# A norm's sum of squares: the last two squares added on VectorE, and the sums one matmul group later

## The chip, the cores and the metric

The kernel runs on one core of one Trainium2 chip. Its engines are TensorE (PE; its weight loads are listed as PEld), VectorE (DVE), ScalarE (ACT), GpSimd (POOL) and SyncE (SP, which here only issues DMAs). The metric is the device time of one execution in microseconds (us), lower being better, as the median of several runs.

## The reference, cut to what matters

The kernel computes a two-layer decoder trunk in float32 for 512 tokens of width 1024. Each layer is a half-step SwiGLU feed-forward, a mixer, and a second half-step feed-forward. Layer 0 mixes with a state-space head group beside an mLSTM head group, layer 1 with sparse attention. Every one of the six stages begins with an RMS norm over the 1024 features of a token.

```python
def rms_norm(x, g):
    xf = x.astype(jnp.float32)
    y = xf * lax.rsqrt(jnp.mean(xf * xf, axis=-1, keepdims=True) + EPS) * g
    return y.astype(x.dtype)

def swiglu(h, w_gate, w_up, w_down):
    return (jax.nn.silu(h @ w_gate) * (h @ w_up)) @ w_down

for l in range(DEPTH):                        # DEPTH = 2
    x = x + 0.5 * swiglu(rms_norm(x, ffn_norm[l, 0]), ...)
    h = rms_norm(x, mix_norm[l])
    m = hybrid_mixer(h, ...) if l % 2 == 0 else sparse_attention(h, ...)
    x = x + m
    x = x + 0.5 * swiglu(rms_norm(x, ffn_norm[l, 1]), ...)
```

## The kernel before, in words

The residual x lives on chip, transposed: `xT` has the features on the 128 partitions in eight chunks (k = 0 to 7) of 512 tokens. Float32 products are made of three matmuls each (`mm3`, lines 241 to 243) over a high and a low part of both operands. Weights come by DMA into a ring of raw buffers; ScalarE and VectorE make their high and low parts ("form", lines 361 and 363), or ScalarE and an accumulating DMA from GpSimd's queue do (lines 391 to 393). TensorE reads the forms and sets the ring free again.

**Stages.** The order is ffn00, mix0, ffn01, ffn10, mix1, ffn11. A feed-forward works on 11 units of 256 hidden features. Its first two units (`unit`) are plain products: eight groups of 12 matmuls of 512 columns. The first four groups take the chunks 0 to 3 (gate, gate, up, up), the last four the chunks 4 to 7. The other units (`unit_seven`) use a seven-product scheme over sums and differences of blocks of x (tile `xf`, made by `xforms`).

**The norm, spread over the end of one stage and the start of the next.** The matmuls of the next stage are begun on x times gain, not yet divided by its root mean square; the division is a multiplication of the results by a row `rrow`. For each of the six norms but the first (which is taken from x as it is loaded), the steps are:

- `prep_later`, called as each pair of chunks of the new x is finished, in the order (0, 1), (2, 3), (6, 7), (4, 5), at the end of mix1 in the order 0 to 7. Per chunk ScalarE makes the high part (line 657), VectorE the low part (line 660) of tile `xgn`, and ScalarE squares the chunk (line 669) into tile `ssq`. GpSimd adds the squares of all but the last pair into one partial sum (through `vtt`, line 356). The squares of the last two chunks stay as they are: with GpSimd's sum there are three partial sums.
- `settle_later`, first call: `sums` (line 327) adds over partitions and over the partial sums with matmuls against a column of ones: for each of the four blocks of 128 tokens one matmul per partial sum, into tile `pssq`. A float32 matmul of this kind is two records in the profile. VectorE then takes the mean (line 624), GpSimd raises it to the power -0.5 (line 626).
- `settle_later`, second call: `rows_of` (line 336, tile `prow`) turns the four columns into a row on every partition, ScalarE copies it to `rrow` (line 630). `xforms` (line 444) and the units' results wait for `rrow`.

**Where the two calls stand.** In `unit` after the second and the fourth group of 12 matmuls (line 600; ffn00 is the "late" case, whose norm has no sums). In mix0 (`unit_eight`) ahead of the second and the third group. In mix1 one call alone, after the first four jobs of the indexer: attention uses the column, not the row.

**The order.** Every step is added to a `Plan` with an engine and an estimated cost; the plan places the steps of the whole kernel by list scheduling (earliest start, then longest way to the end) and so fixes each engine's order. TensorE's steps keep their written order within a stream; only the mixers have several streams, which the plan interleaves. VectorE, ScalarE, GpSimd and SyncE may take later steps first. The plan counts 0.2 + 0.45 us per partial sum for `sums`, and 0.15 + 1.05e-3 us per element of a row for a VectorE step.

Of the kernel before, what the change touches and what calls it, by code (L numbers as in the profile page):

```python
# [13 lines left out]
ALU = mybir.AluOpType  # L14
# [4 lines left out]
NB = T // P  # L19
# [194 lines left out]
class Trunk:  # L214
# [135 lines left out]
    def t(self, us, issue, reads, writes):  # L350
        self.plan.add("tensor", us, issue, reads, writes)
# [224 lines left out]
    def unit(self, raws, stream, late, summed):  # L576

        nc, rrow = self.nc, self.rrow  # L580
        ps = self.pair("pg", "pA"), self.pair("pu", "pB")
        f = []
        for qs in ((0, 1), (2, 3)):
            for i in range(4):
                for _ in range(2 if not f else 1):
                    next(stream, None)
                xg, xgk = self.xg, self.xgk
                if len(f) < 4:
                    f.append(self.made(raws[i], i >= summed))
                j, b = f[i]  # L590
                for s in range(2):
                    col = slice(s * P, (s + 1) * P)
                    for q in qs:
                        k = 2 * q + i % 2
                        self.times(
                            *ps[i // 2], s, (j, lambda b=b, q=q, col=col: (b[:, 0, q, col], b[:, 1, q, col])),
                            lambda k=k: (xg[0][k], xg[1][k]), xgk(k), q == 0 and i % 2 == 0, q == 3 and i % 2 == 1, False, T,
                            0.693,
                        )
                if 2 * qs[0] + i in ((2, 4) if late else (1, 3)):  # L600
                    self.settle_later()
        yield
        t, tk = self.place()
        g = lambda: t()[:, 4:8].rearrange("p (s a) b -> p s (a b)", s=2)
        h = lambda: t()[:, 0:4].rearrange("p (s a) b -> p s (a b)", s=2)
        r = lambda: rrow.unsqueeze(1).to_broadcast([P, 2, T])
        gk, hk = ([tk(a + i) for i in range(4)] for a in (4, 0))
        pk = lambda ps: [(*ps[1], 0), (*ps[1], 1)]
        self.vtt(2 * T, g, ps[0][0], r, ALU.mult, gk, pk(ps[0]) + ["rrow"])
        self.s(2 * T, lambda: nc.scalar.activation(g(), g(), AF.Silu), gk, gk, AF.Silu)  # L610
        self.vtt(2 * T, h, ps[1][0], r, ALU.mult, hk, pk(ps[1]) + ["rrow"])
        self.vtt(2 * T, h, h, g, ALU.mult, hk, hk + gk)
        yield t, tk
# [20 lines left out]
    def prep_later(self, which, k, last, squares=True, half=None):  # L634

        nc = self.nc
        if k == 0 and not half:  # L640
            self.which = which
            self.xgn = [[Lazy(lambda: self.part.tile([P, 4, T], F32R, name="xgn", tag="xg")) for _ in range(2)] for _ in range(2)]
            squares4 = Lazy(lambda: self.tmp.tile([P, 4, T], F32, name="ssq", tag="ssq", bufs=1))
            self.sqs = [lambda i=i: squares4()[:, i] for i in range(4)]
            self.ssq = self.sqs[0]
            self.ssqs, self.ssqk = [(self.ssq, 0)], ["ssq"]
            self.xg = [LazyFeat(t) for t in self.xgn]
            self.xgk = lambda k: [("xg", which, i, k) for i in range(2)]
        xgn, xT, ssq = self.xgn, self.xT, self.ssq
        halves = (0, 1) if half is None else (half,)  # L650
        cols = slice(halves[0] * H, halves[-1] * H + H)
        n = cols.stop - cols.start
        for j in (k, k + 1):
            g, x = self.gain(which, j), xT[:, j, cols]
            hi, lo = (lambda i=i, j=j: xgn[i][j // 4]()[:, j % 4, cols] for i in range(2))
            hik, lok = ([("xg", which, i, j)] for i in range(2))
            self.s(n, lambda hi=hi, x=x, g=g: nc.scalar.activation(hi(), x, AF.Copy, scale=g), self.xk(j, halves), hik)

            def low(hi=hi, lo=lo, x=x, g=g, j=j):
                nc.vector.scalar_tensor_tensor(lo(), x, g, hi().bitcast(F32), op0=ALU.mult, op1=ALU.subtract)  # L660

            self.v(n, low, self.xk(j, halves) + hik, lok)
            if not squares:
                continue
            if j == 0:
                sq, sk = ssq, ["ssq"]
            else:
                sq, sk = self.sqs[1 + j % 3], [("sq", j % 3)]
            self.s(n, lambda x=x, sq=sq: nc.scalar.activation(sq()[:, cols], x, AF.Square), self.xk(j, halves), sk)
            if last:  # L670
                self.ssqs, self.ssqk = self.ssqs + [(sq, halves[0] * NB // 2)], self.ssqk + sk
            elif j:
                part = [lambda x=x: x()[:, cols] for x in (ssq, sq)]
                self.vtt(n, part[0], *part, ALU.add, ["ssq"], ["ssq"] + sk, True)
        if last:
            self.pending = 1 + squares

# [1285 lines left out]
```

## Time and profile before

| what | value |
|---|---|
| median of 3 runs | 2012.17 us (2010.16 to 2013.01) |
| profiled execution, its own time | 2003.96 us |
| span of the profiled execution | 2002.2 us |
| mean granted TensorE clock | 0.992 |
| busy: PE, DVE, ACT, POOL | 1956.5, 1627.8, 1264.7, 325.0 us |
| sums (`pssq`) | 120 records, 14.5 us |
| GpSimd's additions of squares, 128x512 | 22, mean 1551 ns |

The span runs from the first to the last instruction on the core. Busy time of an engine is the time in which one of its instructions ran; "idle before" is time that the engine spent waiting just ahead of an instruction, with the one that released it. The granted clock is the share of TensorE's full rate that its clock gate let through. A line number is the line of the kernel where the instruction was issued; where a helper issues for many places, the tile's name tells them apart.

### The profile page before, as it was taken

The page shows a single profiled execution, that of the slowest core. Times are in us where ns is not written, and L with a number is a line of the kernel's source. Part 1 is how long each engine was busy: PE and PEld are TensorE (multiplying, and loading weights), DVE is VectorE, ACT ScalarE, POOL GpSimd, SP SyncE. Part 2 cuts the span into 40 slices and gives each one's busy share as a digit, 9 for nine tenths or more (in the row PEclk, how much of TensorE's full clock was granted, in tenths as well). Part 3 has the DMA queues.
Part 4 walks back from the last instruction along what each step waited for, and adds up shares of the span by engine and source line. Part 5 has one row for each costly group of instructions (what it writes and reads, how often), then busy time and mean ns, then how long its engine had stood idle before and what let it go on. Part 6 is the DMA issues. An engine that isn't in the chain of part 4 may idle for free.

```text
span 2002.2 us, 36425 instructions
## 1 busy us (share of the span) xinstructions
PE 1956.5 (98%) x14674; PEld 1813.3 (91%) x14674; DVE 1627.8 (81%) x2373; ACT 1264.7 (63%) x1906; POOL 325.0 (16%) x401
## 2 busy tenths in 40 slices
PE   8999999999999999999999999999999999999998
PEld 6999999799888888999998999999866588999998
DVE  6888888887888558989788998878589647988886
ACT  6666656567777545766566566666747744757564
POOL 1000002222234110000012001001414521101010
PEclk9999999999999999999999999999899999999999
DMA  8566766467769342666654466565735202666564
GB/s 221 137 157 152 176 155 161 118 166 190 198 176 262 86 117 74 162 172 162 158 149 141 111 170 161 155 174 137 188 88 116 53 17 69 158 158 169 148 170 115
DMA packets 226609, 292.89 MB, mean 146 GB/s; under 512 B 15036, under 2 KB 196488, under 8 KB 225928
## 3 DMA queue, kind: packets, MB, share of 16 engines
q1 hardware_dynamic: 200728, 199.30, 32.2%
q0 software_dynamic: 25632, 91.24, 24.2%
q8 instruction: 115, 1.88, 0.4%
q14 instruction: 54, 0.44, 0.1%
q10 hardware_dynamic: 80, 0.02, 0.0%
HBM read 192.96 MB, written 6.33 MB: 100 GB/s over the span
## 4 chain that ended last, share of the span: by engine, by line
PE 76%; DVE 8%; DMA 8%; issue 5%; ACT 1%; POOL 1%; SPq 0%; POOLq 0%; ACTq 0%; DVEq 0%
PE pA L242 9%; PE pA L241 9%; PE pA L243 9%; PE pD L241 5%; PE pD L243 5%; PE pD L242 5%; DMA form<-raw 3%; PE hm L242 2%; PE hm L243 2%; PE hm L241 2%; PE pB L241 2%; PE pB L243 2%; PE pB L242 2%; DMA raw<-in_hy_w_in 2%; DVE raw L356 2%
## 5 line engine op out<-in xcount | busy, mean ns | idle before, releaser
L363 DVE TENSOR_TENSOR form<-raw,form 128x1024 fp32r<-128x1024 f32 (+2 forms) x382 | 454.9, 1195 | 101.5 <-ACT form L361 100.0
L361 ACT ACTIVATE form<-raw 128x1024 fp32r<-128x1024 f32 (+2 forms) x382 | 392.1, 1030 | 206.0 <-DVE raw L356 142.4
L392 POOL DMA_DIRECT2D form<-raw x172 | 150.9, 879 | 1344.3 <-ACT form L391 1298.3
L356 DVE TENSOR_TENSOR raw<-raw 128x1024 f32<-128x1024 f32 (+2 forms) x281 | 333.2, 1190 | 22.8 <-DMA raw<-in_ffn_w_down 9.0
L241 PE MATMUL pA<-xf,form 128*128 128x256 f32 x1152 | 321.2, 279 | 0.0
L243 PE MATMUL pA<-xf,form 128*128 128x256 f32 x1152 | 320.7, 278 | 0.0
L242 PE MATMUL pA<-xf,form 128*128 128x256 f32 x1152 | 320.7, 278 | 0.0
L391 ACT ACTIVATE form<-raw 128x1024 fp32r<-128x1024 f32 (+1 forms) x172 | 178.2, 1037 | 161.6 <-PE pD L243 74.4
L241 PEld LDWEIGHTS pA<-xf,form 128*128 128x128 f32 x1152 | 217.2, 188 | 0.3
L243 PEld LDWEIGHTS pA<-xf,form 128*128 128x128 f32 x1152 | 217.3, 189 | 0.0
L242 PEld LDWEIGHTS pA<-xf,form 128*128 128x128 f32 x1152 | 217.0, 188 | 0.2
L242 PE MATMUL pA<-hid,form 128*128 128x256 f32 x704 | 198.2, 282 | 3.3 <-DVE hid L363 3.3
L241 PE MATMUL pA<-hid,form 128*128 128x256 f32 x704 | 198.0, 281 | 0.6 <-ACT hid L361 0.5
L243 PE MATMUL pA<-hid,form 128*128 128x256 f32 x704 | 197.2, 280 | 0.0
L393 ACT ACTIVATE form<-raw 128x1024 fp32r<-128x1024 f32 (+1 forms) x172 | 176.5, 1027 | 0.0
L241 PE MATMUL pD<-xf,form 128*128 128x256 f32 x576 | 160.3, 278 | 0.0
L243 PE MATMUL pD<-xf,form 128*128 128x256 f32 x576 | 160.2, 278 | 0.0
L242 PE MATMUL pD<-xf,form 128*128 128x256 f32 x576 | 160.2, 278 | 0.0
L356 DVE TENSOR_TENSOR ft<-ft 128x256 f32<-128x256 f32 (+2 forms) x296 | 151.3, 543 | 3.6
L242 PEld LDWEIGHTS pA<-hid,form 128*128 128x128 f32 x704 | 132.4, 188 | 5.2 <-DVE hid L363 5.1
L241 PEld LDWEIGHTS pA<-hid,form 128*128 128x128 f32 x704 | 132.6, 188 | 1.4 <-ACT hid L361 0.7
L508 ACT ACTIVATE ft<-pA 128x512 f32<-128x512 f32 x120 | 71.5, 595 | 97.7 <-PE pA L243 90.0
(441 smaller groups left out, 5427.6 us busy)
## 6 DMA issues: line engine op xcount, KB each, us to landing
form<-raw POOLq DMA_DIRECT2D x156, 512.0 KB, 5.9
raw<-in_ffn_w_gate SPq DMA_DIRECT2D x88, 512.0 KB, 3.9
raw<-in_ffn_w_up SPq DMA_DIRECT2D x88, 512.0 KB, 4.1
raw<-in_ffn_w_down SPq DMA_DIRECT2D x64, 512.0 KB, 4.0
raw<-in_hy_w_in SPq DMA_DIRECT2D x44, 512.0 KB, 4.7
raw<-in_ffn_w_down SPq DMA_DIRECT2D x32, 384.0 KB, 3.1
raw<-in_hy_w_out SPq DMA_DIRECT2D x16, 512.0 KB, 4.2
form<-raw POOLq DMA_DIRECT2D x16, 384.0 KB, 4.2
```

The costliest lines, as they stand in the source:

```text
L241: mm(out, l[0], r[0], start=start, stop=False)
L242: mm(out, l[0], r[1], start=False, stop=False)
L243: mm(out, l[1], r[0], start=False, stop=stop)
L356: (self.p if pool else self.v)(n, lambda: e.tensor_tensor(out(), x(), y(), op=op), reads, writes)
L361: self.s(n, lambda: nc.scalar.activation(hi(), src(), AF.Copy), srck, hik)
L363: n, lambda: nc.vector.tensor_tensor(lo(), src(), hi().bitcast(F32), op=ALU.subtract), srck + hik, lok
L391: self.s(n, lambda: nc.scalar.activation(f()[:, 1], raw, AF.Copy, scale=-1.0), rawk, lok)
L392: self.plan.add("gpsimd", 0.85, lambda: nc.gpsimd.dma_start(f()[:, 1], raw, accum_op=ALU.add), rawk + lok, lok, 5.5)
L393: self.s(n, lambda: nc.scalar.activation(f()[:, 0], raw, AF.Copy), rawk, hik)
L508: self.s(T, lambda: nc.scalar.activation(to(), ps()[:, :, 0:H], AF.Copy), [(*psk, 0), (*psk, 1)], tok)
```

## The change

With the last pair, VectorE adds each of the two squares to GpSimd's partial sum as it comes (`vtt` with its last argument false is a VectorE step). `ssqs` then holds one partial sum, and `sums` makes four matmuls in place of twelve, in all five planned norms. In `unit` the first call of `settle_later` moves from after the second group to after the third; the second call stays after the fourth. mix0, mix1 and ffn00 keep the places of their calls.

```diff
@@ unit
-                if 2 * qs[0] + i in ((2, 4) if late else (1, 3)):
+                if 2 * qs[0] + i in ((2, 4) if late else (2, 3)):
                     self.settle_later()
@@ prep_later
             self.s(n, lambda x=x, sq=sq: nc.scalar.activation(sq()[:, cols], x, AF.Square), self.xk(j, halves), sk)
-            if last:
-                self.ssqs, self.ssqk = self.ssqs + [(sq, halves[0] * NB // 2)], self.ssqk + sk
-            elif j:
+            if j:
                 part = [lambda x=x: x()[:, cols] for x in (ssq, sq)]
-                self.vtt(n, part[0], *part, ALU.add, ["ssq"], ["ssq"] + sk, True)
+                self.vtt(n, part[0], *part, ALU.add, ["ssq"], ["ssq"] + sk, not last)
```

## The prediction

> **What bounds the kernel now.** I read the page's busy line and the chain that ended last first, to see whose time counts.
>
> ```profile
> PE 1956.5 (98%) x14674; PEld 1813.3 (91%) x14674; DVE 1627.8 (81%) x2373; ACT 1264.7 (63%) x1906; POOL 325.0 (16%) x401
> ...
> PE 76%; DVE 8%; DMA 8%; issue 5%; ACT 1%; POOL 1%; SPq 0%; POOLq 0%; ACTq 0%; DVEq 0%
> ```
>
> TensorE (PE) is busy 98% of the span and carries 76% of the chain. The other engines feed it through rings of buffers that PE itself sets free, so time taken out of PE's queue should move the end, unless a feeder is late afterwards. VectorE (DVE) at 81% is the next candidate.
>
> Next PE in order of time around the sums of the five planned norms (tile pssq) and the row transposes (prow) that follow; the first row is the tile's own (min/median/max ns), each other one is from a stretch of its own: start, us, instruction, and in brackets PE's wait ahead of it. I call the norms A (mix0), B (ffn01), C (ffn10), D (mix1), E (ffn11).
>
> ```profile
> L327 PE MATMUL pssq<-raw,ssq x120: 164/250/352, 359.1 to 1664.4; 128*128 128x1 f32 x120
> 359.12 2.73 PE L327 MATMUL pssq<-raw,ssq 128*128 128x1 f32 x24
> 366.14 0.38 PE L336 MATMUL prow<-raw 128*128 128x128 f32 x2
> 750.17 2.73 PE L327 MATMUL pssq<-raw,ssq 128*128 128x1 f32 x24
> 758.36 0.49 PE L336 MATMUL prow<-raw 128*128 128x128 f32 x3
> 1085.14 2.74 PE L327 MATMUL pssq<-raw,ssq 128*128 128x1 f32 x24
> 1093.30 0.38 PE L336 MATMUL prow<-raw 128*128 128x128 f32 x2
> 1429.89 2.73 PE L327 MATMUL pssq<-raw,ssq 128*128 128x1 f32 x24
> 1432.88 0.40 PE L241 MATMUL gm<-iw,xgn 128*128 128x292 f32 x1 [0.25 <-DVE raw L624]
> 1661.16 3.55 PE L327 MATMUL pssq<-raw,ssq 128*128 128x1 f32 x24 [0.88 <-POOL ssq L356]
> 1672.62 0.38 PE L336 MATMUL prow<-raw 128*128 128x128 f32 x2
> ```
>
> The 12 matmuls of a norm (four token blocks, three partial sums) are 24 records, 2.73 us. The last record lasts 0.25 us and overlaps what follows, so one costs PE (2.73 - 0.25) / 23 = 0.108 us. E took 3.55 us after a wait of 0.88 for GpSimd. And the same work after the sums is not equally long: from their end to prow B has 24 matmuls of 512 columns in 758.36 - 752.90 = 5.46 us, C 5.42, but E 24 in 1672.62 - 1664.71 = 7.91, and A 12 in 366.14 - 361.85 = 4.29 (half of 5.46 is 2.73). So I asked for the granted clock in windows of 3.41 us, the length of the drops, all instructions first:
>
> ```profile
> core 0: us, PE busy (x) PEld busy (x) DVE busy (x) ACT busy (x) POOL busy (x), PEclk, DMA share, GB/s
> 359.19:362.60 3.41, 3.41 (x29) 3.27 (x28) 0.34 (x2) 0.00 (x0) 0.48 (x1) 1.00 0.98 304
> 362.60:366.01 3.41, 3.41 (x10) 2.62 (x9) 0.00 (x0) 0.00 (x0) 0.56 (x1) 0.50 0.19 47
> 1430.97:1434.38 3.41, 3.16 (x26) 3.07 (x27) 0.22 (x2) 0.45 (x3) 1.03 (x1) 1.00 1.09 189
> 1434.38:1437.80 3.42, 2.63 (x12) 2.28 (x11) 2.85 (x8) 1.57 (x5) 2.22 (x2) 0.50 0.95 257
> 1437.80:1441.21 3.41, 3.41 (x17) 3.39 (x15) 1.52 (x2) 1.65 (x3) 3.41 (x8) 0.50 1.04 396
> 1659.67:1663.08 3.41, 2.54 (x24) 2.33 (x22) 2.60 (x5) 2.83 (x5) 1.43 (x1) 1.00 0.41 138
> 1663.08:1666.49 3.41, 3.41 (x14) 3.02 (x14) 0.61 (x2) 0.00 (x0) 1.02 (x1) 0.50 0.02 5
> 1666.49:1669.90 3.41, 3.41 (x10) 2.64 (x9) 0.00 (x0) 0.00 (x0) 0.00 (x0) 0.50 0.00 0
> 611.77:615.18 3.41, 1.08 (x10) 0.88 (x8) 3.41 (x3) 3.41 (x8) 3.33 (x4) 1.00 1.06 281
> 615.18:618.60 3.42, 3.20 (x21) 2.87 (x22) 3.42 (x4) 2.05 (x3) 2.11 (x2) 0.50 1.03 329
> ```
>
> The same windows for pssq alone (length, PE, PEld and VectorE busy, granted clock, DMA share, GB/s):
>
> ```profile
> 359.19:362.60 3.41, 2.66 (x24) 2.57 (x23) 0.16 (x1) 1.00 0.98 304
> 748.29:751.71 3.42, 1.54 (x15) 1.72 (x15) 0.00 (x0) 1.00 0.05 8
> 1086.18:1089.60 3.42, 1.70 (x16) 1.61 (x15) 0.16 (x1) 1.00 0.85 270
> 1430.97:1434.38 3.41, 1.66 (x15) 1.57 (x15) 0.16 (x1) 1.00 1.09 189
> 1659.67:1663.08 3.41, 1.92 (x18) 1.93 (x18) 0.00 (x0) 1.00 0.41 138
> ```
>
> Read together: in a window in which one-column sums and waits of PE fill 2.66 us (A), 1.66 + 0.25 = 1.91 (D) or 1.92 + 0.87 = 2.79 (E), the next stretch is granted half the clock. Where they fill 1.54 (B) or 1.70 (C), nothing follows: B's and C's 24 matmuls took 5.46 and 5.42. A plain wait does the same (611.77: 2.33 idle, then 0.50). So, as a reading of these rows: over about half a window of one-column matmuls or waiting costs at least one window at half speed. Sums of 2.73 us can do that alone if they lie in one window.
>
> **The change part by part.**
>
> *Sums of 4 instead of 12 matmuls, five times.* 16 records less: 16 x 0.108 = 1.73 us per norm, 5 x 1.73 = 8.6 us, all PE time. In E the last six records ran at half speed; there the sums go from 3.55 to about 8 x 0.108 + 0.14 = 1.0, some 0.8 more: 9.4 together.
>
> *The half-clock windows after the sums.* Shortened sums fill 0.9 us of 3.41, far under the 1.70 that did nothing. A gets back 4.29 - 2.73 = 1.6, E 7.91 - 5.42 = 2.5. In D both windows hold 2.63 + 3.41 = 6.04 us of PE work at half speed, so at most 3.0 comes back; at least 0, since PE waits there for other engines too; I take 2.0, nearer to the upper end since PE is full in the second window. Together 6.1.
>
> *Two additions per norm on VectorE.* Priced by the same operation of the same size, 0.69 us (first row: its group, busy us and mean ns; then rows in order of time from A and C):
>
> ```profile
> L356 DVE TENSOR_TENSOR ft<-ft 128x512 f32<-128x512 f32 x112 | 73.8, 686 | 1.0
> 356.72 2.34 DVE L363 TENSOR_TENSOR form<-raw,form 128x1024 fp32r<-128x1024 f32 x2
> 357.04 0.62 ACT L669 ACTIVATE ssq<-raw 128x512 f32<-128x512 f32 x1
> 1087.91 0.16 DVE L624 TENSOR_SCALAR raw<-pssq 128x4 f32<-128x4 f32 x1
> 1088.15 1.47 POOL L626 TENSOR_TENSOR raw<-raw 128x4 f32<-128x4 f32 x1 [5.58 <-DVE raw L624]
> ```
>
> Ten of them are 6.9 us of VectorE. They wait for GpSimd's last addition and for the last square, and the sums now wait for them. Behind them on VectorE stand the low parts of the last chunks and the next weight forms, which PE needs one group (2.73 us) later or more. In A the position of the sums stays: the last square ends at 357.66, VectorE does two forms until 359.06, PE wants the sums at 359.12. If the planner puts the addition between the forms it costs nothing; behind both, 359.06 + 0.69 - 359.12 = 0.63 us. I take half, 0.3. In D the low parts are long done and VectorE idles, so nothing. In the feed-forwards the sums come 12 matmuls (2.73 us) later, which covers 2 x 0.69; in E this also removes the 0.88 us wait for GpSimd, since PE goes on with the third group: -0.9. Without that cover each feed-forward would pay up to 1.4.
>
> *Sums a group later in B, C, E.* No DMA and no new instruction moves: the matmuls, the VectorE step L624 and GpSimd's L626 come later, in no queue of SP. prow stays where it is, so the cover of the chain from sums to prow falls from 24 matmuls (5.46) to 12 (2.73). The slowest chain seen is C: the sums end at 1087.88, L626 at 1088.15 + 1.47 = 1089.62, 1.74 us. That leaves 1.0 us of slack. If L624 stands behind one form of 1.17 us (half of 2.34), PE waits 0.2; behind two, 1.4. Behind a waiting prow stands the second half of the unit. I take 0.2 for each of three: +0.6, range 0 to 4.2.
>
> *Sum:* -9.4 - 6.1 - 0.9 + 0.3 + 0.6 = -15.5 us. Norm A's gain (3.4) comes ahead of mix0's waits for weights; the feeders are released by PE and should move with it, but I leave half of it out as absorbed: +1.5. Forecast **-14 us**. The sum belongs to the profiled execution (span 2002.2, its own time 2003.96); the median of the runs shown, 2012.17, lies 8.2 above, and I carry the difference over: 2012.17 - 14 = **1998.2 us**.
>
> [...]
>
> **The rivals.**
>
> 1. *Only the matmuls go.* The windows lie anywhere against the program; in the timed runs the sums may straddle two windows as B and C do here, or the removed drop reappears at the next wait. For it: two of five norms show no drop. Against: the three others do. Time: -9.4 - 0.9 + 0.9 = -9.4, 2002.8. [...]
>
> 2. *The mixers absorb it.* PE's lead in A and D ends at the next transfer or VectorE chain. Then only B, C and E count: 2 x 1.73 + 1.73 + 0.9 - 0.6 = -5.5, 2006.7. For it: the waits below; against: those feeders wait for buffers that PE sets free.
>
> 3. *The shorter cover is too short.* L624 or the additions stand behind two forms in B, C and E, 1.4 us each, and drops stay elsewhere: -9.4 - 0.9 + 0.3 + 4.2 = -5.8 at worst; with two additions late by 1.4 each time as well, -1.6, 2010.6: no change.
>
> 4. *Slower: the planner draws another order.* It places every step by its own costs; it counts 1.55 us for the sums before and 0.65 after, and has ten more steps to place, so its clock shifts by about 0.9 us per norm. In the mixers several PE streams interleave by that clock, and there PE's longest waits stand:
>
> ```profile
> PE hc L1308 <- DVE rw L1297: 4.9, 2, 2.6
> ...
> PE hm L243 <- DMA form<-raw: 4.0, 4, 1.5
> PE pq L1521 <- DVE q L1511: 3.7, 2, 3.0
> PE gm L242 <- DVE iw L363: 3.4, 1, 3.4
> ```
>
> These are 16.0 us, and the waits over 2.3 us cost a half-speed window (1.7) each. A worse order that doubles them adds 16.0 + 3 x 1.7 = 21: 2012.17 - 14 + 21 = 2019. It decides from 14 + 4 = 18 us of new waits. Against it: PE's order in the feed-forwards is written, and a lead common to all streams leaves their order alone.
>
> **How the numbers follow.** Forecast 0.47, rival 1 0.25, rival 2 0.11, rival 3 0.09, rival 4 0.08. A measurement of this kernel can tell about 0.2%, 4 us. Forecast, rivals 1 and 2 are faster: 0.83; rival 3 is the same, 0.09; rival 4 slower, 0.08. The forecast's own range is 1994 to 2001 (D's window 0 to 3, A's gain whole or half, prow's waits). With rivals 1 and 2 and most of 3 it reaches up to 2009; down to 1992, if in the timed runs four or five norms lose a window.
>
> **What would show it.** Right: pssq x40, about 0.9 us a norm; granted clock 1.00 in the windows after each; 24 matmuls between sums and prow become 12 with prow not waiting; no wait for ssq in E; two more VectorE additions of 0.69 us per norm. Wrong: a wait of prow on L626 or of pssq on VectorE over 1 us, half-clock windows at other places in equal number, or longer waits in mix0 and mix1 than the 16 us above.

## The result, and the profile after

The changed kernel is faster by 0.8%: median 1995.55 us (13 runs, 1990.74 to 2002.94) against 2013.01 for the kernel before on the same chip (13 runs, 1998.89 to 2017.5), ratio 0.992 with a 95% interval of 0.9902 to 0.9937. The forecast was 1998.2 us, 14 us less than before.

The profiled executions differ by less: spans 2002.2 and 1993.7, that is 8.5 us. The one before is low among its own runs (2003.96, median 2013.01), the one after is at its median. One pair of traces thus shows half of the gain; the other half has to be looked for in all runs.

The page after, busy line and chain:

```profile
PE 1948.8 (98%) x14594; PEld 1804.3 (91%) x14594; DVE 1630.4 (82%) x2383; ACT 1267.8 (64%) x1906; POOL 320.5 (16%) x401
...
PE 78%; DVE 7%; DMA 6%; issue 5%; ACT 2%; POOL 1%; POOLq 0%; ACTq 0%; DVEq 0%; SPq 0%
```

TensorE has 80 records less and is still busy 98%; VectorE has ten more, all of them in one row below. Next the tiles' own rows (min/median/max ns), and PE in order of time at the five sums and the row transposes, as it was shown for before:

```profile
L327 PE MATMUL pssq<-raw,ssq x40: 164/250/271, 360.5 to 1659.4; 128*128 128x1 f32 x40
L356 DVE TENSOR_TENSOR ssq<-ssq x10: 678/688/693, 359.0 to 1657.9; 128x512 f32<-128x512 f32 x10
360.55 1.02 PE L327 MATMUL pssq<-raw,ssq 128*128 128x1 f32 x8 [1.10 <-DVE ssq L356]
364.30 0.60 PE L336 MATMUL prow<-raw 128*128 128x128 f32 x4
753.92 0.95 PE L327 MATMUL pssq<-raw,ssq 128*128 128x1 f32 x8
757.58 0.60 PE L336 MATMUL prow<-raw 128*128 128x128 f32 x4
1089.21 0.95 PE L327 MATMUL pssq<-raw,ssq 128*128 128x1 f32 x8
1092.87 0.60 PE L336 MATMUL prow<-raw 128*128 128x128 f32 x4
1430.83 0.95 PE L327 MATMUL pssq<-raw,ssq 128*128 128x1 f32 x8
1658.63 1.05 PE L327 MATMUL pssq<-raw,ssq 128*128 128x1 f32 x8 [2.89 <-DVE ssq L356]
1663.96 0.49 PE L336 MATMUL prow<-raw 128*128 128x128 f32 x3
```

The sums went from 3 x 2.73 + 2.74 + 3.55 = 14.48 us to 1.02 + 3 x 0.95 + 1.05 = 4.92. No prow row has a bracket: the shorter cover holds. A and E have new waits for VectorE's additions, 3.99 us together, where before had 0.88 in E alone. Both are longer than 1 us, which the prediction had named as a sign of being wrong. From the end of the sums to prow it is 12 matmuls now: 364.30 - 361.57 = 2.73 in A, 2.71 in B and C, but 1663.96 - 1659.68 = 4.28 in E. The granted clock says why (length, busy us and count of PE, PEld, DVE, ACT and POOL, granted clock, DMA share, GB/s):

```profile
362.60:366.01 3.41, 3.41 (x19) 2.79 (x18) 0.44 (x1) 0.60 (x1) 0.30 (x1) 1.00 0.53 175
1433.50:1436.90 3.40, 2.67 (x21) 2.44 (x20) 2.83 (x8) 2.85 (x7) 2.15 (x2) 1.00 1.01 310
1657.10:1660.52 3.42, 1.89 (x12) 1.75 (x13) 2.77 (x6) 1.05 (x2) 0.47 (x1) 1.00 0.00 0
1660.52:1663.93 3.41, 3.41 (x9) 2.54 (x8) 0.00 (x0) 0.00 (x0) 0.55 (x1) 0.50 0.00 0
612.62:616.03 3.41, 2.67 (x13) 2.45 (x13) 3.41 (x7) 1.23 (x2) 0.42 (x1) 0.50 0.94 231
1083.66:1087.08 3.42, 3.42 (x10) 2.68 (x9) 3.38 (x6) 2.38 (x4) 0.00 (x0) 0.50 0.47 153
```

The drops after the sums of A and D are gone. E has one window left, now after a wait. Drops at waits have grown elsewhere: the one at 612 holds four windows here, 13.65 us, where before's held one, 3.42, and one at 1083.66 is new. So in this pair of executions the mean clock is almost the same, 0.992 and 0.993. Over all runs it is not, as the next part shows. The waits of PE that matter (total us, times, longest):

```profile
PE hm L243 <- DMA form<-raw: 5.5, 4, 2.0
PE pssq L327 <- DVE ssq L356: 4.0, 2, 2.9
PE pA L243 <- DVE form L363: 3.4, 1, 3.4
PE hc L1306 <- DVE rw L1295: 3.2, 2, 2.1
PE pg L242 <- DVE xgn L660: 2.5, 3, 1.0
PE hc L242 <- DVE xgn L660: 1.8, 2, 1.0
...
PE pq L1519 <- ACT ri L1531: 0.7, 1, 0.7
```

Before's wait of 3.7 us of `pq` for VectorE's q is no longer there: the only `pq` row left has 0.7. Near its 3.4 of `gm` for VectorE (at 1416) there is one of the same length for `pA L243` (at 1413). All PE waits over 0.15 us add up to 40.6 us in the trace of before and 39.3 after: the 3.1 us lost at the sums came back elsewhere, above all in the mixers, whose streams the planner interleaves differently now.

### The profile page after: what moved, and what is told of

Read it like the earlier page. It is cut to its first block, busy times and chain, and to the rows that moved or that the text cites. A ratio compares the mean times of both kernels' runs of the same rounds, so it can differ in the third digit from the quotient of the medians.

```text
span 1993.7 us, 36269 instructions
## 1 busy us (share of the span) xinstructions
PE 1948.8 (98%) x14594; PEld 1804.3 (91%) x14594; DVE 1630.4 (82%) x2383; ACT 1267.8 (64%) x1906; POOL 320.5 (16%) x401
## 4 chain that ended last, share of the span: by engine, by line
PE 78%; DVE 7%; DMA 6%; issue 5%; ACT 2%; POOL 1%; POOLq 0%; ACTq 0%; DVEq 0%; SPq 0%
PE pA L242 9%; PE pA L243 9%; PE pA L241 9%; PE pD L243 5%; PE pD L241 4%; PE pD L242 4%; PE hm L241 3%; PE hm L243 3%; PE hm L242 3%; DMA form<-raw 3%; PE pB L241 2%; PE pB L243 2%; PE pB L242 2%; DVE form L363 2%; PE pu L241 2%
## 5 line engine op out<-in xcount | busy, mean ns | idle before, releaser
L243 PE MATMUL pA<-xf,form 128*128 128x256 f32 x1152 | 321.1, 279 | 0.0
L243 PEld LDWEIGHTS pA<-xf,form 128*128 128x128 f32 x1152 | 217.3, 189 | 0.1
L243 PE MATMUL pA<-hid,form 128*128 128x256 f32 x704 | 197.4, 280 | 3.4 <-DVE form L363 3.4
L243 PE MATMUL pD<-xf,form 128*128 128x256 f32 x576 | 160.3, 278 | 0.4 <-DMA form<-raw 0.4
L242 PEld LDWEIGHTS pA<-hid,form 128*128 128x128 f32 x704 | 132.6, 188 | 5.2 <-DVE hid L363 5.1
L243 PEld LDWEIGHTS pA<-hid,form 128*128 128x128 f32 x704 | 132.8, 189 | 3.6 <-DVE form L363 3.6
L241 PEld LDWEIGHTS pA<-hid,form 128*128 128x128 f32 x704 | 132.8, 189 | 1.9 <-ACT hid L361 0.8
```

Of the source, the lines that this page charges most:

```text
L241: mm(out, l[0], r[0], start=start, stop=False)
L242: mm(out, l[0], r[1], start=False, stop=False)
L243: mm(out, l[1], r[0], start=False, stop=stop)
```

## The experiments

Two theories stood against each other. **T1**: the gain is PE's: 16 one-column records less per norm, plus the half-clock windows that such records bring. **T2**: the gain is a luckier order, drawn by the planner because the step costs less in its account; the records hardly count. Within T1, clock and records were to be separated, and the parts of the change from each other.

Each run of a kernel has its own mean granted clock, to three places. "Lost" is (1 - mean clock) x mean time, "rest" is the mean time less that, an estimate of the time at full clock. (It takes a half-clock window to cost half its length, although PE also waits in some.) The 76 runs of before that stand beside the experiments give 0.9903, lost 19.5, rest 1991.9. By the scatter of the runs, a difference in lost or rest between two rows is known to some 2 us, with six runs or fewer to 3 or 4.

| kernel | median us (runs) | ratio to before, 95% | clock | lost | rest |
|---|---|---|---|---|---|
| changed | 1995.55 (13) | 0.992 (0.9902 to 0.9937) | 0.9927 | 14.6 | 1981.7 |
| e1 before again | 2010.63 (12) | 1.0001 (0.998 to 1.0023) | 0.9900 | 20.1 | 1991.9 |
| e2 additions only | 1996.41 (6) | 0.9921 (0.9893 to 0.995) | 0.9942 | 11.6 | 1984.7 |
| e3 later place only | 2010.98 (12) | 0.9986 (0.9967 to 1.0006) | 0.9907 | 18.8 | 1991.0 |
| e4 before, 128 columns | 2000.97 (9) | 0.9948 (0.9925 to 0.9971) | 0.9951 | 9.8 | 1991.8 |
| e5 changed, matmuls tripled | 2015.24 (12) | 1.0013 (0.9997 to 1.0029) | 0.9888 | 22.7 | 1991.8 |
| e6 changed, 128 columns | 1996.47 (6) | 0.9907 (0.9882 to 0.9932) | 0.9948 | 10.3 | 1984.8 |
| e7 all additions VectorE | 1995.79 (6) | 0.9915 (0.9891 to 0.9939) | 0.9920 | 16.0 | 1980.8 |
| e8 e7, 128 columns | 1992.75 (5) | 0.9898 (0.9876 to 0.9921) | 0.9944 | 11.2 | 1982.2 |
| e9 changed again | 1997.13 (10) | 0.9938 (0.9917 to 0.996) | 0.9937 | 12.6 | 1983.8 |
| e10 calls at (3, 5) | 2011.22 (12) | 1.0000 (0.9976 to 1.0023) | 0.9908 | 18.4 | 1992.4 |
| e11 e10, mix0 later, 128 columns | 2011.93 (12) | 1.0010 (0.9988 to 1.0033) | 0.9905 | 19.1 | 1992.2 |
| e12 calls at (4, 6), else e11 | 2011.57 (12) | 1.0009 (0.9985 to 1.0033) | 0.9915 | 17.1 | 1994.9 |

**e1, before again** (unchanged, a control).

> The kernel before, unchanged, to see the granted clock of each of its runs (of the changed kernel's 13 runs the mean granted clock is 0.9927, so about 14.6 us at full speed are lost to half-clock windows). Theory 1 (fewer records and fewer half-clock windows): the records give 8.6 us, the other 8 us or so of the measured gain are the clock; then the mean granted clock of these runs is about 0.989 and the slow runs are those with the low clock. Theory 2 (fewer records and a luckier order of the planner, clock not involved): the mean granted clock is the same 0.993 within 0.001, and the gain beyond 8.6 us stands in PE's waits. Ratio to the kernel before: 1.000 in both.

Ratio 1.0001. The clock, 0.9900, is nearer to T1's 0.989 than to T2's 0.993. Its trace also has what the first trace of before lacked, a drop after the sums of B and of C:

```profile
751.70:755.11 3.41, 3.41 (x26) 3.19 (x26) 1.77 (x8) 0.00 (x0) 1.01 (x1) 1.00 0.54 159
755.11:758.52 3.41, 3.41 (x9) 2.65 (x9) 3.07 (x11) 0.00 (x0) 0.52 (x3) 0.50 0.00 0
1089.60:1093.00 3.40, 3.40 (x26) 3.24 (x27) 1.89 (x5) 0.00 (x0) 0.75 (x1) 1.00 0.70 233
1093.00:1096.40 3.40, 3.40 (x9) 2.65 (x9) 0.97 (x1) 0.00 (x0) 0.72 (x1) 0.50 0.35 102
```

Here the sums of B (751.09 to 753.82) lie in one window but for 0.61 us, while in the first trace they straddled two (1.54 in the one shown). So the norms that pay differ between two executions of one kernel.

**e2, additions only**: the changed kernel with the first call back after the second group.

```diff
-                if 2 * qs[0] + i in ((2, 4) if late else (2, 3)):
+                if 2 * qs[0] + i in ((2, 4) if late else (1, 3)):
```

> One part of the change alone: VectorE adds the last two squares (four matmuls per norm instead of twelve), but in the feed-forwards the sums stay after the second group. Theory 1: the records and the clock give nearly all, minus the waits of PE for VectorE's additions in ffn01, ffn10 and ffn11, about 1 to 1.5 us each: 12 to 14 us faster than before (ratio about 0.9935). Theory 2: another order again, anything between -8 and -16, with the clock equal to the kernel before's.

0.9921: not told apart from the whole change. Its clock, 0.9942, is not before's, as T2 had it. Its sums wait 1.10 (A), 1.64 (C) and 2.57 (E). Its rest, by 6 runs, is 3.0 us longer than that of the changed kernel's first runs (1981.7) and 0.9 longer than that of its second (1983.8): no difference is shown.

**e3, later place only**: before with the first call after the third group, three partial sums kept.

```diff
-                if 2 * qs[0] + i in ((2, 4) if late else (1, 3)):
+                if 2 * qs[0] + i in ((2, 4) if late else (2, 3)):
```

> The other part alone: three partial sums and twelve matmuls as before, the sums one group later in the feed-forwards. Theory 1: records and half-clock windows stay, so within 3 us of the kernel before (ratio 0.9985 to 1.001). Theory 2: if the place in the order brought the gain beyond the records, about 8 us faster (ratio 0.996).

0.9986, no difference shown, as T1 forecast; T2's 8 us (0.996) lie outside the interval. In its trace E waits 0.87 us for GpSimd's addition, as before.

**e4, before with wide sums**: the twelve matmuls per norm stay, each against 128 columns of ones in place of one; the first of each 128 equal columns is read. It computes the same. The edit, shortened at the dots:

```diff
-                    ps[:, b : b + 1], x[...], self.ones1, ...
+                    ps[:, b * w : (b + 1) * w], x[...], self.ones[:, 0:w], ...       # w = 128
-            self.v(4, lambda: nc.vector.tensor_scalar(ms, ps()[:, 0:NB], ...
+            self.v(4, lambda: nc.vector.tensor_scalar(ms, ps()[:, 0:T:P], ...
```

> The kernel before, with the sums' matmuls made 128 columns wide instead of one (the same 24 records per norm, every column of the result the same sum, the mean read from each 128th column). It changes how busy the sums keep the array, not how many records there are. Theory 1, with the reading that one-column matmuls count as idle for the clock: no half-clock window begins right after the sums, the mean granted clock rises by about 0.003 and the time falls by about 5 to 8 us even if a record takes a little longer (ratio about 0.997). Theory 2, or the reading that only a PE without instructions lowers the clock: clock as before, and the time the same or longer by what the wider records cost (0 to 15 us).

The tile's row, A's sums and prow, and A's windows:

```profile
L327 PE MATMUL pssq<-raw,ssq x120: 270/275/377, 360.1 to 1662.4; 128*128 128x128 f32 x120
360.12 2.84 PE L327 MATMUL pssq<-raw,ssq 128*128 128x128 f32 x24
365.57 0.60 PE L336 MATMUL prow<-raw 128*128 128x128 f32 x4
359.19:362.60 3.41, 3.41 (x28) 3.22 (x27) 1.06 (x2) 0.99 (x2) 0.00 (x0) 1.00 0.92 285
362.60:366.01 3.41, 3.41 (x21) 2.85 (x20) 0.16 (x1) 0.00 (x0) 1.04 (x1) 1.00 0.52 161
```

Twenty-four records with 128 times the products take 2.84 us instead of 2.73, PE is as busy (3.41 of 3.41), and no drop follows; A's twelve matmuls after the sums take 2.61 us, against 4.29. The rest is before's (1991.8; before has 1991.0 on the same chip and 1991.9 over all its runs), the lost time falls from 20.6 (the 26 runs of before on the same chip) to 9.8: -10.8 us by the clock, at equal records, with PE's order as in before (its `pq` wait of 3.7 is still there). T1 had forecast 5 to 8 us and a clock 0.003 higher; T2 can't produce this.

By the profile PE was busy 3.41 of 3.41 us in A's window in both traces, before's and this one. The next window got 0.50 in the one and 1.00 in the other, and the edit between them is the width of the matmuls.

**e5, changed, matmuls tripled**: the four matmuls are done three times into columns of their own, and the last four are read: 24 records per norm again, with additions and places as changed. It computes the same. The edit, shortened to the loop:

```diff
-        for b in range(NB):
+        for r in range(3):
+            for b in range(NB):
+                c = r * NB + b                 # column c; columns 8 to 11 are read
```

> The changed kernel with its four one-column matmuls per norm done three times (24 records again, as before the change; the third result is used). Additions, place and planner's costs stay those of the changed kernel, so only the records return. Theory 1 (records and clock make the gain): nearly all of it goes, 8.6 us for the records and about 6 for half-clock windows: back to the kernel before within 4 us (ratio 0.998 to 1.001), mean granted clock 0.990. Rival (the additions' place in the planner's order makes half of the gain): 6 to 9 us stay (ratio about 0.996).

2015.24: the gain is gone, all of it, as T1 forecast. Rest 1991.8, as before; lost 22.7. Drops are back after the sums of A, shown here, and of C (its windows, from 1093.60 on, have 1.00 and 0.50 as well):

```profile
359.70:363.10 3.40, 3.40 (x27) 3.22 (x27) 0.94 (x4) 0.00 (x0) 0.75 (x1) 1.00 0.32 94
363.10:366.50 3.40, 3.40 (x11) 2.56 (x10) 0.00 (x0) 0.00 (x0) 0.30 (x1) 0.51 1.05 355
```

The planner was told the same cost as in the changed kernel, and its waits over 0.15 us add up to the same (39.5 us against 39.3). So T2 falls: with that account and the old number of records no gain is left (0.9997 to 1.0029).

**e6, changed and wide** (e4's edit on the changed kernel).

> The changed kernel with its eight records per norm 128 columns wide. Theory 1: the sums themselves no longer count as idle, and what is left of half-clock windows is from real waits of PE (1.1 us in mix0 and 2.9 us in ffn11 at the sums themselves, and the waits in the mixers); mean granted clock 0.9927 to about 0.994, 2 to 4 us under the changed kernel (ratio 0.990 to 0.991). Rival (eight short records are already too short to lower the clock): the same as the changed kernel, ratio 0.992.

0.9907, within the changed kernel's interval, and its own interval holds both forecasts. The lost time, 10.3 against 14.6 and 12.6 us, points to T1, but six runs don't show it. What width still saves at 8 records per norm stays open.

**e7, all additions on VectorE**: GpSimd adds no squares at all.

```diff
-                self.vtt(n, part[0], *part, ALU.add, ["ssq"], ["ssq"] + sk, not last)
+                self.vtt(n, part[0], *part, ALU.add, ["ssq"], ["ssq"] + sk)
```

> The changed kernel with all additions of squares on VectorE, none on GpSimd (28 more VectorE additions of 0.69 or 0.42 us, some 18 us busy). Theory of contention: VectorE's low parts of x took 1.77 us while GpSimd added and 0.74 otherwise, and PE waits about 3.5 us for them in mix0 and ffn10 and 4.0 us at the sums for the chain of additions; both shrink, and 4 to 6 us under the changed kernel (ratio about 0.9895). Rival (VectorE, 82% busy, becomes the bound at the ends of stages): PE's waits for VectorE stay or grow, 0 to 4 us over the changed kernel (ratio 0.992 to 0.994).

0.9915, not told apart from the changed kernel; both forecasts lie within its interval. Sums wait longer:

```profile
PE pssq L327 <- DVE ssq L356: 6.4, 3, 2.5
...
PE pg L242 <- DVE xgn L660: 1.0, 1, 1.0
```

That is 2.4 us more than in the changed kernel, while the waits for low parts of `xgn` (line 660) fell from 2.5 + 1.8 to 1.0 + 0.7. In this trace the one pays for the other.

**e8, all on VectorE and wide.**

> Both: all additions on VectorE and the sums' records 128 columns wide. If contention and the clock of the sums are two separate costs, their gains add: 6 to 10 us under the changed kernel (ratio 0.987 to 0.989), mean granted clock about 0.995. If the waits were the only thing left that lowers the clock, the same as with all additions on VectorE alone.

The lowest median, 1992.75, but five runs, and an interval (0.9876 to 0.9921) that overlaps the changed kernel's. It is not shown to be better, and whether the two gains add stays open.

**e9, changed again** (beside e10 to e12, on their chip).

> The changed kernel once more, as the mark for the three beside it: ratio 0.990 to 0.994, mean granted clock about 0.993.

0.9938 (0.9917 to 0.996), as the first time. Beside 33 runs of before on the same chip (lost 18.3, rest 1992.5) it loses 12.6 with a rest of 1983.8: -5.7 by the clock, -8.7 by work.

**e10, both calls two groups later**, to take E's wait away: sums after the fourth group, row after the sixth.

```diff
-                if 2 * qs[0] + i in ((2, 4) if late else (2, 3)):
+                if 2 * qs[0] + i in ((2, 4) if late else (3, 5)):
```

> The changed kernel with the sums of the feed-forwards after the fourth group of matmuls and the row transposes after the sixth. In ffn11 PE waits 2.9 us at the sums since the third group is drawn ahead of the last attention matmuls. Theory (the chain from the last residual to the sums has a fixed length and only matmuls placed between them cover it): the wait in ffn11 falls from 2.9 to under 0.5 us, and the half-clock window after it goes; 3 to 5 us under the changed kernel. Rival (the planner draws the fourth group ahead too, or the later row holds up what waits for it): the wait stays near 2.9, the same time as the changed kernel within 2 us, or up to 3 us slower.

A miss for both: 2011.22, 14 us behind the changed kernel. The rival had named what happens, a later row that holds up what waits for it, but at 3 us at most. E still waits 2.9. And the row came later: prow of B at 763.78, not 757.58. The waits of PE, and what led to the first of them, in order of time (ACT, DVE, PE), with two windows:

```profile
PE pA L241 <- ACT ft L508: 9.0, 3, 3.1
PE pssq L327 <- DVE ssq L356: 5.9, 3, 2.9
763.78 0.60 PE L336 MATMUL prow<-raw 128*128 128x128 f32 x4
797.87 3.09 DVE L363 TENSOR_TENSOR xf<-ft,xf 128x512 fp32r<-128x512 f32 x5
799.79 0.60 ACT L508 ACTIVATE ft<-pA 128x512 f32<-128x512 f32 x1 [0.59 <-DVE xf L363]
800.45 0.39 PE L241 MATMUL pA<-xf,form 128*128 128x256 f32 x1 [2.97 <-ACT ft L508]
798.10:801.50 3.40, 1.05 (x9) 1.06 (x10) 3.30 (x6) 2.19 (x4) 0.00 (x0) 1.00 0.62 116
801.50:804.90 3.40, 3.40 (x19) 3.40 (x18) 3.40 (x4) 1.06 (x1) 0.00 (x0) 0.50 0.10 11
```

`xforms` waits for the row. VectorE's last low parts of `xf` run from 797.87 to 800.96 (in the changed kernel they end at 796.12); ScalarE, which copies the first seven-product result out of `pA` (line 508), waits for a buffer that they read; and PE, 37 us after prow, waits 2.97 us for that copy. The wait is followed by a half-clock window. It happens in all three feed-forwards: 9.0 us. PE's waits over 0.15 us add up to 50.8 us, 11.5 more than in the changed kernel, and the rest is 8.6 us longer than e9's on the same chip; the remaining 5.8 of the 14.4 between the mean times is lost clock.

**e11: as e10, with mix0's calls one group later (`i in (2, 3)`) and e4's width. e12: as e11 with (4, 6).**

> As the kernel with the sums after the fourth group, and in mix0 the two calls one group later as well, and the records 128 columns wide. Theory: the waits at the sums (1.1 in mix0, 2.9 in ffn11) both go, and so does what the sums cost in clock: 5 to 9 us under the changed kernel, ratio 0.988 to 0.990. Rival: the waits move to the row or stay; ratio 0.991 to 0.993.

> The same with the sums of the feed-forwards after the fifth group, which reads the last chunks' own parts, and the row after the seventh. Theory: no wait at the sums can be left, for the fifth group itself waits for the same chunks; but the row comes 5 us later for what waits for it, so not better than the sums after the fourth group: ratio 0.988 to 0.991. Rival (the row's lateness costs PE): 2 to 5 us slower than that one.

Both at before's time, 1.0010 and 1.0009: every ratio forecast for them, 0.988 to 0.993, was missed. In e11 A's wait at the sums is gone and the three waits for the copies stay; in e12 no sums wait, but PE waits for ScalarE's copies (6.4 us) and for VectorE's `xf` (2.7). PE's waits add up to 51.5 and 52.1 us, against 39.3 in the changed kernel: the later row costs more than the sums can give.

## Why the prediction was right, and where it was not

**The records: right.** 16 less per norm were to give 8.6 us, 9.4 with E's half-speed ones; the sums measure 14.48 - 4.92 = 9.56 less. That PE time moves the end is shown by e5, which puts the records back and returns to a rest of 1991.8; the changed kernel's, over its 23 runs (its own and e9), is 1982.6, 9.3 below before's.

**The half-clock windows: right in cause and in sum, wrong in place.** The forecast was 6.1 us in A, D and E. Over the same 23 runs 13.7 us are lost, over before's 76 runs 19.5: -5.8; on e9's chip alone it is -5.7. That the one-column shape brings the drops was read from one trace and is shown by e4; that about half a window of it is needed was not tested by itself, and one window of the trace after speaks against it: A's wait of 1.10 and sums of 1.02 lie in 359.19:362.60 (PE busy 2.31 of 3.41), 2.12 us together, more than D's 1.91 in before, and the next window has 1.00. But the norms do not pay by a fixed list: B and C lost windows in e1, and in the profiled execution after, waits at 612 and 1083 took windows that the sums had left. That the sums agree is luck in part: the 6.1 was read from one execution, and e4 puts what the narrow sums cost over all runs at some 10 us (9.8 lost against 19.5), of which the changed kernel got 5.8 back. In its trace E's sums, after a wait of 2.89, are still followed by a drop; whether that and A's wait make up the remainder is not shown. Rival 1, "only the matmuls go", at -9.4, is what the pair of profiles alone would seem to say (-8.5); the runs' clocks (0.9927, 0.9942 and 0.9937 in the changed kernel, e2 and e9, against 0.9903) speak against it, and the interval, 12.7 to 19.7 us, leaves -9.4 out.

**E's wait of 0.88 us removed: this step failed.** It grew to 2.89. The step assumed that the third group, put ahead of the sums, would cover the additions. VectorE and GpSimd in the changed kernel, then PE's `pu` (third group) and `lg` (the last product of attention's output) alone in two stretches:

```profile
1653.15 3.48 POOL L356 TENSOR_TENSOR ssq<-ssq 128x512 f32<-128x512 f32 x2 [7.21 <-ACT ssq L669]
1655.78 0.42 DVE L356 TENSOR_TENSOR raw<-lg,raw 128x256 f32<-128x256 f32 x1 [0.28 <-PE lg L243]
1656.21 0.96 DVE L660 SCALAR_TENSOR_TENSOR xgn<-raw,xgn 128x512 fp32r<-128x512 f32 x1
1657.10 1.48 DVE L356 TENSOR_TENSOR ssq<-ssq 128x512 f32<-128x512 f32 x2
1648.25:1651.16 2.91, 2.91 (x12) 2.07 (x11) 0.00 (x0) 1.00 0.64 196
1651.16:1655.74 4.58, 4.58 (x39) 4.38 (x38) 1.26 (x3) 0.00 (x0) 1.00 0.18 43
```

The planner spent the third group's 12 matmuls (first stretch, `pu`) ahead of the last `lg` matmuls (second stretch), on which the squares depend. So after the last `lg` nothing was left for PE, and the chain of residual, square, low part and two additions, 1655.74 to 1658.63, stands bare. PE's order within a stream is written; between mix1's streams and ffn11's first groups it is not, although the text ahead of the prediction gives several streams to the mixers alone. The trace of before already has the overlap, there with the second group (`pg`) ahead of the last `lg`:

```profile
1655.22 0.39 PE L243 MATMUL pg<-xgn,form 128*128 128x512 f32 x1
1655.44 0.28 PE L241 MATMUL lg<-oh,form 128*128 128x256 f32 x1
```

The experiments part the two halves of the change here: the later place alone leaves the wait at 0.87 (e3), the additions alone make it 2.57 (e2). In C the cover did what the prediction said: the additions alone make PE wait 1.64 (e2), with the later place it does not wait.

**A's addition, 0.3 us: the term of the sum was too small, 1.10 measured.** The forecast's bound put one addition behind two forms, 0.63. VectorE has both behind three, so that PE gets the sums 1.10 us late:

```profile
355.59 3.48 DVE L363 TENSOR_TENSOR form<-raw,form 128x1024 fp32r<-128x1024 f32 x3
359.00 1.41 DVE L356 TENSOR_TENSOR ssq<-ssq 128x512 f32<-128x512 f32 x2
```

**prow's cover, +0.6: not needed.** In the trace after no prow waits, in any norm.

**Half of A's gain absorbed, +1.5: not borne out as such.** What balanced the losses at the sums (3.1 us) was the `pq` wait of 3.7 that the new order removed. The prediction had rival 4 look at this list of waits for harm alone; the redrawn order changed it, and in sum it did no harm: 40.6 and 39.3 us. So the -14 rests on two right terms, records and clock, and on two misses that another shift made good by chance.

**Rivals 2 and 3** are excluded by the interval and by prow's rows. Rival 2's sum left out what its own premise keeps, E's window (2.5) and half-speed records (0.8); with them it gives -8.8, outside the interval too. Rival 3's mechanism, a row that comes too late, is real all the same: two groups later it costs the whole gain (e10), though at another place than prow.

## What to carry to other kernels

In these traces very narrow matmuls cost more than their time: a dozen in a row were followed by a window at 0.50 where they filled 2.66 us of one window of 3.41 (A in before), and by none where they filled 1.54 or 1.70 (B and C); D, with 1.66 and a wait of 0.25, had one. Eight records in place of 24, or 24 of 128 columns, were followed by 1.00 in A. So add partial sums on another engine first, or, where the records must stay, make them wider (e4: 2.84 us in place of 2.73, and 9.8 us of clock lost in place of 20.6). Before a step of a chain is moved later, follow its end to the farthest consumer: here the row's lateness showed 37 us on, in a buffer's release. And compare the clocks of all runs, not of one pair of traces, before a difference is put down to drops.

## What the hardware showed that was not expected

A float32 matmul against 128 columns took PE hardly longer here than one against a single column: 24 records 2.84 us (e4) and 2.73 (before), single records 275 and 250 ns in the median.

Why some drops last one window and others two or four stays open: in the trace after, PE was busy 3.42 of 3.42 us in the window from 616.03 on, within the drop at 612, and the next one was at 0.50 again.

The spread of an unchanged kernel's runs is mostly its clock: over the 76 runs of before, from 0.984 to 0.995, the time goes with the mean granted clock at 2.0 us per 0.001, which is what (1 - clock) x 2011 gives. The drops differ between the executions traced (B and C have one in e1 and none in the first), and a change worth less than 4 us is not told apart here by some ten runs.
